# The first stream columns loaded ahead of the last conditioning weights, and the sums of squared keys and queries taken one stream step later

## The chip, the core and the metric

The kernel runs on one core of one Trainium2 chip. The metric is the device time of one execution in microseconds (us). Five engines work side by side, each with a queue of its own: TensorE (PE: matmuls and transposes into PSUM), VectorE (DVE), ScalarE (ACT), GpSimd (POOL) and SyncE (SP, which here issues most of the loads). A semaphore orders two engines where one reads what the other wrote.

## What is computed

One step of a decoder layer for 512 prompt tokens and 8 single tokens of other sequences (520 columns in all), width 1024, in fp32. The part that the change touches:

```
mod  = c @ w_ada + b_ada                       # conditioning: shifts, scales, gates (6 x 1024)
h    = rmsnorm(x, norm1_g) * (1 + sc1) + sh1
proj = h @ w_in                                # q, kv, gates, DeltaNet q/k/v, z, a, b, merge
y    = silu(causal_conv4(DeltaNet q/k/v of proj))
q, k = l2norm(q), l2norm(k)                    # x * rsqrt(sum(x*x) + eps), per head of 128
g    = -exp(a_log) * softplus(a + dt_bias);  beta = sigmoid(b)
o_dn = chunked gated delta rule(q, k, v, g, beta)
o_nsa = native sparse attention (compressed, selected and window branches)
x    = x + gt1 * ((gate_a * o_nsa + gate_b * o_dn) @ w_out)
x    = x + gt2 * (relu(rmsnorm2(x) @ w_up)^2 @ w_down);  then a final rmsnorm
```

## The kernel before, in words

**The stream.** All large products with w_in, w_out, w_up and w_down are cut into units of 128 columns of the weight. A unit is a load of 512 KB (`raw`, `w_load`, L348, issued by SyncE at L351), a rounding on ScalarE (`wh`, L397), a residual on VectorE (`wl`, L401) and two halves of matmuls: the tokens are two halves of 256 and 264 columns, and for each half and each of the eight slices of 128 rows TensorE adds hh·wh, hl·wh and hh·wl (hh and hl are the rounded and the residual part of the normalised input), 24 matmuls into one bank `pg` of PSUM. `load_upto` (L373) issues loads, `split_upto` makes wh and wl, and each call of `step()` first lets every unit in flight go on by one `yield` (`advance()`) and then adds one half to the program. Units in order: two of k_cmp (the first is group 0), the gates, four keys of DeltaNet (k0 to k3), two of v_cmp, keys k4 to k7, eight values, eight queries (q0 to q7), and so on.

**A key or query unit** (`conv`, L556, then `ev_k`, L595, or `ev_q`, L622). Its two halves are copied from PSUM by ScalarE into `pre` (L496); ScalarE multiplies the first tap into `cy` (L565), VectorE adds three taps (L567), ScalarE takes a tanh into `pre` (L569), VectorE makes the silu (L571), and ScalarE squares it into `pre` (L597 for keys, L624 for queries). `norms` (L576) then sums the squares over the 128 rows by four small matmuls (`quarters`; in the profile under L169, `bek<-pre,consts`) into a bank that four heads share; for each fourth head it copies the bank (L587), transposes it, adds EPS on VectorE (L592) and takes the power −1/2 on GpSimd (L593). `pre` and `cy` come from four buffers of one tag (`e2`, L107), with some smaller users.

**Conditioning.** w_ada comes in chunks, two loads of 512 KB a chunk (`ada_load`, L243, issued at L251). The first sixteen are chained: each is issued in SyncE's queue behind the one before (`tc.issue_after(starts[-1].ins)`), and the first stream load behind the sixteenth. `ada` multiplies the conditioning vectors with a chunk (`quarters` again, under L169 as `bek<-wa,consts`), ScalarE copies the result (`ma`, L261), and a second step (`rest`) brings it into `mod` (L267). `modulate` then makes hh and hl of two slices each.

**What sets the order.** A planner lays the queue of each engine: it simulates the program in time and takes what is ready, in the order of the code where several things are, with priorities for some. The place in the code is so a wish and not the order itself.

The loop over the chunks, and what follows it:

```python
    fetch(3)
    for j in range(8):
        ...
        rest.append(ada(i, was[i]))
        fetch(j + 4 if j < 5 else 8)
        ...
    load_upto(0)
    split_upto(0)
```

Of the kernel before, what the change touches and what calls it, by code (L numbers as in the profile page):

```python
# [69 lines left out]
def hybrid_step(ctx: ExitStack, tc: tile.TileContext, A, O, dbg=None):  # L70


    nc = tc.nc
# [19 lines left out]
    def kb4(pool, shape, dt, name, tag, bufs=None):  # L93
        x = pool.tile([128, 2 * SLOT], dt, name=name, tag=tag, **({} if bufs is None else dict(bufs=bufs)))
        n = 1
        for v in shape:
            n *= v
        x = x[:, 0:n]
        return x if len(shape) == 1 else x.rearrange("p (a b) -> p a b", a=shape[0])
# [79 lines left out]
    for hf in range(2):  # L179
        c = slice(hf * 512, hf * 512 + 512)  # L180
        nc.sync.dma_start(crow[hf][0:1], A["c_prompt"][:, c])
        starts = [nc.sync.dma_start(crow[hf][1:9], A["c_sample"][:, c])]
# [62 lines left out]
    def ada_load(j0, hf, pool=None):  # L245
        if pool is None:
            wa = kb4(wp, (4, 256,), F32, "wa", "wraw", bufs=NRAW)
        else:
            wa = kb4(pool, (4, 256,), F32, "wa", "q4")
        with tc.issue_after(starts[-1].ins) if len(starts) < 17 else nullcontext():  # L250
            r = nc.sync.dma_start(wa, w_ada[:, hf * 4:hf * 4 + 4, j0 * 256:j0 * 256 + 256])  # L251
        if len(starts) < 17:
            starts.append(r)
        return wa

    def ada(j0, wa):

        pa = bank("ek")
        quarters(pa[:, 0:256], lambda j, s: cT[:, 18 * j + 9 * s:18 * j + 9 * s + 32], lambda j, s: wa[j // 2][:, j % 2 * 2 + s], True, True, 2)
        ma = e2("ma")[:, 0:256]  # L260
        nc.scalar.copy(out=ma, in_=pa[:, 0:256])  # L261

        def rest():
            pt = bank("ek")
            for hf in range(2):
                mm(pt[:, hf * 16:hf * 16 + 9], ma[:, hf * 128:hf * 128 + 128], sel, start=True, stop=True)
            nc.vector.tensor_tensor(mod[:, 2 * j0:2 * j0 + 2], pt[:, 0:32].rearrange("p (b n) -> p b n", b=2)[:, :, 0:9],  # L267
                                    vec[:, 16 + 2 * j0:18 + 2 * j0, None].to_broadcast([128, 2, 9]), op=ALU.add)
        return rest
# [27 lines left out]
    def norm1(t):  # L297
        n = x_rows(t)[1]
        xt = x_tile(t)
        nc.vector.tensor_scalar(xt[0:n], xt[0:n], ssq[0:n, t:t + 1], None, op0=ALU.mult)  # L300
        for hf in range(2):
            x_transposed(xnT, xt[:, hf * 512:(hf + 1) * 512], t, hf * 4, "sc" if hf else "pt")
# [38 lines left out]
    pos = {"unit": 0, "half": 0, "split": 0, "load": 0}  # L341
# [6 lines left out]
    def w_load(ap):  # L348
        def load():
            raw = kb4(wp, (KT, 128,), F32, "raw", "wraw", bufs=NRAW)  # L350
            nc.sync.dma_start(raw, ap)  # L351
            return raw
        return load

# [18 lines left out]
    def load_upto(g):  # L373
        while pos["load"] <= min(g, len(groups) - 1):
            x = groups[pos["load"]]
            with tc.issue_after(starts[-1].ins) if pos["load"] == 0 else nullcontext():
                x.raw = x.load()
            pos["load"] += 1

    def split_upto(u):  # L380
        while pos["split"] <= u and pos["split"] < len(units):
            un = units[pos["split"]]
            if "ada" in un and pos["split"] > pos["unit"]:
                return
            load_upto(un["g"])
            if un.get("same"):
                un["w"] = un["same"]["w"]
            elif "ada" not in un:
                raw = groups[un["g"]].raw
                if un.get("keep"):  # L390
                    wh, wl = (kb4(wp, (KT, 128,), F32R, "wk", "wkeep", bufs=NKEEP) for _ in range(2))
                else:
                    wh = kb4(wp, (KT, 128,), F32R, "wh", "wh")
                    wl = kb4(wp, (KT, 128,), F32R, "wl", "wl")
                if un["on"] == "scalar":
                    with tc.issue_after(slot["mixed"].ins) if un.get("keep") else nullcontext():
                        nc.scalar.copy(out=wh, in_=raw)  # L397
                else:
                    (nc.vector if un["on"] == "vector" else nc.gpsimd).tensor_copy(wh, raw)
                kp = KT - WLP  # L400
                nc.vector.tensor_tensor(wl[:, 0:kp], raw[:, 0:kp], f32(wh[:, 0:kp]), op=ALU.subtract)  # L401
                if WLP:
                    nc.gpsimd.tensor_tensor(wl[:, kp:], raw[:, kp:], f32(wh[:, kp:]), op=ALU.subtract)
                un["w"] = wh, wl
                load_upto(un["g"] + 2)
            pos["split"] += 1
# [152 lines left out]
    def conv(ct, P, out=None):  # L559

        pre, y = e2("pre"), e2("cy")[:, 0:S]
        nc.vector.memset(pre[:, 0:3], 0.0)
        yield from copies(pre[:, 3:523], P)
        nc.vector.tensor_copy(tail[:, ct], pre[:, 512:523])
        nc.scalar.activation(y, pre[:, 0:S], AF.Copy, scale=cw[:, 0, ct:ct + 1])  # L565
        for j in range(1, 4):
            nc.vector.scalar_tensor_tensor(y, pre[:, j:j + S], cw[:, j, ct:ct + 1], y, op0=ALU.mult, op1=ALU.add)  # L567
        e = pre[:, 0:S]
        nc.scalar.activation(e, y, AF.Tanh)  # L569
        out = y if out is None else out  # L570
        nc.vector.scalar_tensor_tensor(out, e, 1.0, y, op0=ALU.add, op1=ALU.mult)  # L571
        return out, e
# [4 lines left out]
    def norms(i, out, sq):  # L577

        h = i % 4
        if h == 0:  # L580
            norm_bank[0] = bank("ek")
        p = norm_bank[0]
        quarters(p[:, 0:128], lambda j, s: one_of[:, 31 - h:63 - h], lambda j, s: sq[:, j * 128:j * 128 + 128], h == 0, h == 3)
        if h < 3:
            return
        e = e2("nrm")[:, 0:128]
        nc.scalar.copy(out=e, in_=p[:, 0:128])  # L587
        yield
        p = bank("ek")
        tr(p[:, 0:128], e, ident)  # L590
        t = wk.tile([128, 4, 4], F32, name="nsq", tag="nsq", bufs=2)
        nc.vector.tensor_scalar(t, p[:, 0:128].rearrange("p (c h) -> p h c", c=4)[:, 0:4], EPS, None, op0=ALU.add)  # L592
        nc.gpsimd.tensor_tensor(out, t, mhalf.rearrange("p (h c) -> p h c", h=4), op=ALU.pow)  # L593

    def ev_k(i, P):  # L595
        y, e = yield from conv(8 + i, P, slot["kT"][:, i])
        nc.scalar.activation(e, slot["kT"][:, i], AF.Square)  # L597
        yield
        yield
        hs = slice(i - 3, i + 1)  # L600
        r = lns[:, :, hs].rearrange("p c h -> p h c")
        yield from norms(i, r, e)
        if i % 4 == 3:
            nc.vector.tensor_tensor(brk[:, hs], r, slot["beta"][:, :, hs].rearrange("p c h -> p h c"), op=ALU.mult)
            nc.vector.tensor_tensor(brk2[:, :, hs].rearrange("p c h -> p h c"), r, brk[:, hs], op=ALU.mult)
# [16 lines left out]
    def ev_q(i, P):  # L622
        y, e = yield from conv(i, P, slot["qT"][:, i])
        nc.scalar.activation(e, y, AF.Square)  # L624
        yield
        yield
        hs = slice(i - 3, i + 1)
        r = rq2[:, hs]
        yield from norms(i, r, e)
        if i % 4 == 3:  # L630
            nc.vector.tensor_scalar(rq[:, hs], r, float(128 ** -0.5), None, op0=ALU.mult)
            nc.vector.tensor_tensor(r, rq[:, hs], rq[:, hs], op=ALU.mult)
# [95 lines left out]
    g_in("dnk0", C_DN + 1024, 512, ev_k)  # L728
    g_in("v_cmp", C_KV + 256, 256, kv_cmp(2), when("X2"))
    g_in("dnk1", C_DN + 1536, 512, lambda i, P: ev_k(4 + i, P))  # L730
    g_in("dnv", C_DN + 2048, 1024, ev_v, when("bv"))
    g_in("dnq", C_DN, 1024, ev_q, when("bv"))
# [27 lines left out]
    def fetch(n):  # L760

        for j in range(len(was), n):
            i = j // 2 + 4 * (j % 2)
            was[i] = [ada_load(i, 0, q4), ada_load(i, 1, None if j % 4 == 3 else q4)]
# [4 lines left out]
    for j in range(8):  # L769
        if j < 5:  # L770
            norm1(j)
        i = j // 2 + 4 * (j % 2)
        rest.append(ada(i, was[i]))
        fetch(j + 4 if j < 5 else 8)
        if j % 2:
            for r in rest:
                r()
            rest = []
            if j < 4:
                continue  # L780
            for i in range(j // 2 if j > 5 else 0, j // 2 + 1):
                modulate(xnT, 0, 0, 8, hh, hl, 2 * i, 2 * i + 2)
            if j == 5:
                slot["early"] = slot["rest"]
# [1215 lines left out]
```

## Time and profile before

| | us |
|---|---|
| median of three runs | 1309.7 (1305.91 to 1313.38) |
| the profiled execution | 1307.84 |
| its span in the profile | 1306.1 |
| TensorE busy | 1216.6 (93%) |
| VectorE busy | 843.8 (65%) |
| ScalarE busy | 647.2 (50%) |
| GpSimd busy | 230.1 (18%) |

The profile is that of one execution. A row of a view "in order of time" gives the start (us from the beginning of the span), the duration, the engine, the line, the operation, what it writes and reads, and, in brackets, how long the engine sat idle ahead of it and whose end ended that. `bpg` are the banks of the stream, `bek` banks for conditioning, norms and transposes. In a list of stretches PEclk is the clock granted to TensorE as a share of 2.4 GHz: 0.5 is 1.2 GHz.

### The profile page before, as it was taken

How to read it: one execution, taken by the hardware profiler on the slowest of the kernel's cores; microseconds unless marked ns; L12 is line 12 of the kernel's file. 1: busy time of each engine (PE TensorE's matmuls, PEld its weight loads, DVE VectorE, ACT ScalarE, POOL GpSimd, SP SyncE). 2: the span in 40 equal slices, each digit the busy share in tenths (PEclk: the TensorE clock that was granted, in tenths of full speed). 3: DMA queues.
4: the chain of work that ended last, by engine and by line, in shares of the span. 5: the costliest groups of instructions: out<-in, count | busy, mean ns of one | idle time of the engine just before them, and what ended most of it. 6: DMA issues, size and time to landing. Idle time of an engine off the chain costs nothing. (4 is left out here: it accounts for less than half of the span.)

```text
span 1306.1 us, 26716 instructions
## 1 busy us (share of the span) xinstructions
PE 1216.6 (93%) x10356; PEld 1150.1 (88%) x10356; DVE 843.8 (65%) x2291; ACT 647.2 (50%) x1561; POOL 230.1 (18%) x323
## 2 busy tenths in 40 slices
PE   4899899999888999799998899999999999999997
PEld 3788889989788999678887798989999999999996
DVE  4576958795357788787777787896834334334355
ACT  4565857654243336656646677574643132232244
POOL 2112100112111111312221323230431021020000
PEclk9899989999699999899999899999999999999999
DMA  8852412425613345346344222371732332332533
GB/s 273 216 156 74 126 32 51 119 78 151 182 47 108 103 130 146 98 116 197 99 116 136 74 72 85 94 196 33 210 95 69 98 95 83 97 97 83 161 90 105
DMA packets 234834, 149.82 MB, mean 115 GB/s; under 512 B 9290, under 2 KB 230018, under 8 KB 234444
## 3 DMA queue, kind: packets, MB, share of 16 engines
q1 hardware_dynamic: 224804, 134.77, 36.4%
q0 software_dynamic: 2240, 6.38, 1.8%
q10 hardware_dynamic: 7664, 6.97, 1.8%
q8 instruction: 81, 1.33, 0.4%
q14 instruction: 45, 0.37, 0.1%
HBM read 136.87 MB, written 15.60 MB: 117 GB/s over the span
## 5 line engine op out<-in xcount | busy, mean ns | idle before, releaser
L153 PE MATMUL bpg<-hh,wh 128*128 128x256 f32 (+1 forms) x1168 | 342.2, 293 | 1.2 <-ACT hh L1521 0.7
L153 PE MATMUL bpg<-hh,wl 128*128 128x256 f32 (+1 forms) x1168 | 337.5, 289 | 2.0 <-DVE wl L401 2.0
L153 PE MATMUL bpg<-hl,wh 128*128 128x256 f32 (+1 forms) x1168 | 337.7, 289 | 0.0
L153 PEld LDWEIGHTS bpg<-hh,wh 128*128 128x128 f32 x1168 | 225.2, 193 | 5.2 <-issue 2.0
L153 PEld LDWEIGHTS bpg<-hh,wl 128*128 128x128 f32 x1168 | 224.5, 192 | 4.0 <-DVE wl L401 2.5
L153 PEld LDWEIGHTS bpg<-hl,wh 128*128 128x128 f32 x1168 | 225.5, 193 | 1.5 <-issue 0.8
L401 DVE TENSOR_TENSOR wl<-raw,wh 128x1024 fp32r<-128x1024 f32 x149 | 183.0, 1229 | 65.7 <-ACT wh L397 60.3
L397 ACT CAST wh<-raw 128x1024 fp32r<-128x1024 f32 x117 | 121.6, 1048 | 181.9 <-PE bpg L153 174.5
L153 PE MATMUL bpg<-act,wh 128*128 128x264 f32 (+1 forms) x1024 | 186.5, 284 | 0.0
L153 PEld LDWEIGHTS bpg<-act,wh 128*128 128x128 f32 x1024 | 157.7, 188 | 0.1
L153 PE MATMUL bpg<-act,wl 128*128 128x264 f32 (+1 forms) x512 | 145.0, 284 | 0.2 <-DVE wl L401 0.2
L153 PE MATMUL bpg<-h2h,wh 128*128 128x256 f32 (+1 forms) x448 | 126.7, 283 | 0.0
L153 PE MATMUL bpg<-h2h,wl 128*128 128x256 f32 (+1 forms) x448 | 126.6, 282 | 0.0
L153 PE MATMUL bpg<-h2l,wh 128*128 128x256 f32 (+1 forms) x448 | 126.3, 282 | 0.0
L1848 POOL TENSOR_TENSOR r<-r 128x520 f32<-128x520 f32 (+2 forms) x40 | 54.1, 1354 | 291.2 <-ACT r L1847 291.2
L1811 DVE SCALAR_TENSOR_TENSOR o_dn<-bpg,consts,o_dn 128x256 f32<-128x256 f32 x80 | 38.3, 484 | 100.3 <-PE bpg L153 100.3
L153 PEld LDWEIGHTS bpg<-act,wl 128*128 128x128 f32 x512 | 96.5, 189 | 0.5 <-DVE wl L401 0.4
L153 PEld LDWEIGHTS bpg<-h2h,wl 128*128 128x128 f32 x448 | 84.4, 188 | 0.3 <-DVE wl L401 0.2
L153 PEld LDWEIGHTS bpg<-h2l,wh 128*128 128x128 f32 x448 | 84.4, 188 | 0.0
L153 PEld LDWEIGHTS bpg<-h2h,wh 128*128 128x128 f32 x448 | 84.3, 188 | 0.0
L153 PE MATMUL bsp<-K,qst 128*128 128x288 f32 (+6 forms) x288 | 68.9, 317 | 5.5 <-DVE consts L267 2.3
L1851 DVE TENSOR_TENSOR act<-r,act 128x520 fp32r<-128x520 f32 (+2 forms) x40 | 23.6, 590 | 73.4 <-ACT act L1850 73.3
(634 smaller groups left out, 2453.3 us busy)
## 6 DMA issues: line engine op xcount, KB each, us to landing
raw<-in_w_in SPq DMA_DIRECT2D x68, 512.0 KB
wa<-in_w_ada SPq DMA_DIRECT2D x48, 512.0 KB
raw<-in_w_down SPq DMA_DIRECT2D x40, 512.0 KB
raw<-in_w_up SPq DMA_DIRECT2D x36, 512.0 KB
raw<-in_w_out SPq DMA_DIRECT2D x12, 512.0 KB
Sx<-in_state_dn SPq DMA_DIRECT2D x16, 256.0 KB
out_s_dn<-Sx SPq DMA_DIRECT2D x16, 256.0 KB
pg<-in_cache_k_slc SPq DMA_DIRECT2D x16, 128.0 KB
```

Of the source, the lines that this page charges most:

```text
L153: nc.tensor.matmul(out, lhs, rhs, start=start, stop=stop)
L397: nc.scalar.copy(out=wh, in_=raw)
L401: nc.vector.tensor_tensor(wl[:, 0:kp], raw[:, 0:kp], f32(wh[:, 0:kp]), op=ALU.subtract)
L1811: nc.vector.scalar_tensor_tensor(xi[:, q], p[:, 0:n], mod[:, m + i, 0:1], xi[:, q], op0=ALU.mult, op1=ALU.add)
L1848: nc.gpsimd.tensor_tensor(r, r, r, op=ALU.mult)
L1851: nc.vector.tensor_tensor(b_, r, f32(a), op=ALU.subtract)
```

## The change

Two edits. The first moves the load of group 0 in SyncE's queue: it is issued within the loop over the chunks, after `fetch(7)` at j = 3, and takes a place of its own in the chain of the w_ada loads, so that the last two of the sixteen (the halves of the eighth chunk to be fetched) are issued behind it. The split of that unit stays where it was. The second puts one more `yield` ahead of `norms` in `ev_k` and `ev_q`, so that what `norms` issues stands one call of `step()` (half a unit of the stream) later in the program; the squares themselves stay.

```diff
     def w_load(ap):
         def load():
             raw = kb4(wp, (KT, 128,), F32, "raw", "wraw", bufs=NRAW)
-            nc.sync.dma_start(raw, ap)
+            with tc.issue_after(starts[-1].ins) if pos["load"] == 0 else nullcontext():
+                r = nc.sync.dma_start(raw, ap)
+            if pos["load"] == 0:
+                starts[-1] = r
             return raw
         return load
...
             x = groups[pos["load"]]
-            with tc.issue_after(starts[-1].ins) if pos["load"] == 0 else nullcontext():
-                x.raw = x.load()
+            x.raw = x.load()
             pos["load"] += 1
...
         nc.scalar.activation(e, slot["kT"][:, i], AF.Square)
         yield
         yield
+        yield
         hs = slice(i - 3, i + 1)
...
         nc.scalar.activation(e, y, AF.Square)
+        yield
         yield
         yield
...
         fetch(j + 4 if j < 5 else 8)
+        if j == 3:
+            load_upto(0)
         if j % 2:
```

## Rows read from the trace of the kernel before

**Rows 1.** The page's head and its part on engines: busy us, share, instructions.
```profile
span 1306.1 us, 26716 instructions
...
PE 1216.6 (93%) x10356; PEld 1150.1 (88%) x10356; DVE 843.8 (65%) x2291; ACT 647.2 (50%) x1561; POOL 230.1 (18%) x323
```

**Rows 2.** Waits of TensorE, 0 to 75 us: total us, times, longest.
```profile
PE bek L169 <- DMA wa<-in_w_ada: 8.0, 5, 2.9
```

**Rows 3.** Waits of TensorE, 75 to 360 us.
```profile
PE bek L169 <- ACT pre L597: 5.4, 3, 2.5
...
PE bek L169 <- ACT pre L624: 2.2, 1, 2.2
...
PE bsp L160 <- PE bek L169: 0.7, 1, 0.7
```

**Rows 4.** Stretches: us, busy by engine (x count), PEclk, DMA share, GB/s.
```profile
37.00:48.00 11.00, 8.18 (x44) 6.87 (x45) 6.56 (x17) 5.10 (x10) 0.00 (x0) 0.53 1.05 249
48.00:60.00 12.00, 12.00 (x103) 12.00 (x102) 5.97 (x17) 7.92 (x17) 3.01 (x3) 1.00 0.48 130
85.00:89.00 4.00, 4.00 (x23) 3.97 (x21) 4.00 (x11) 2.40 (x4) 1.05 (x1) 0.57 0.32 83
...
140.00:160.00 20.00, 16.13 (x126) 15.02 (x124) 19.46 (x46) 17.42 (x40) 1.83 (x2) 0.91 0.37 105
```

**Rows 5.** SyncE, 27 to 46 us in order of time: start, us, what.
```profile
27.40 5.50 SPq L251 DMA_DIRECT2D wa<-in_w_ada  x6
32.95 4.01 SPq L351 DMA_DIRECT2D raw<-in_w_in  x2
```

**Rows 6.** TensorE, 24 to 49 us in order of time, idle time before in brackets.
```profile
32.58 1.07 PE L169 MATMUL bek<-wa,consts 128*32 128x256 f32 x16 [1.17 <-DMA wa<-in_w_ada]
...
35.85 1.07 PE L169 MATMUL bek<-wa,consts 128*32 128x256 f32 x16 [1.10 <-DMA wa<-in_w_ada]
39.82 1.94 PE L169 MATMUL bek<-wa,consts 128*32 128x256 f32 x16 [2.90 <-DMA wa<-in_w_ada]
...
43.41 0.56 PE L153 MATMUL bpg<-hh,wh 128*128 128x256 f32 x1
```

**Rows 7.** ScalarE and VectorE, 35 to 50 us in order of time.
```profile
42.10 1.05 ACT L397 CAST wh<-raw 128x1024 fp32r<-128x1024 f32 x1
...
43.18 1.22 DVE L401 TENSOR_TENSOR wl<-raw,wh 128x1024 fp32r<-128x1024 f32 x1 [0.26 <-ACT wh L397]
```

**Rows 8.** Norms on TensorE, from its order of time around each.
```profile
102.33 0.42 PE L169 MATMUL bek<-pre,consts 128*32 128x128 f32 x8 [1.37 <-ACT pre L597]
...
263.02 0.42 PE L169 MATMUL bek<-pre,consts 128*32 128x128 f32 x8
...
291.41 0.42 PE L169 MATMUL bek<-pre,consts 128*32 128x128 f32 x8 [2.21 <-ACT pre L624]
```

**Rows 9.** TensorE, 74 to 85 us in order of time.
```profile
75.80 0.28 PE L153 MATMUL bpg<-hh,wh 128*128 128x256 f32 x1
...
84.20 0.43 PE L169 MATMUL bek<-pre,consts 128*32 128x128 f32 x8 [2.50 <-ACT pre L597]
```

**Rows 10.** TensorE's groups by shape, 63.9 to 84 and 269 to 291.7 us.
```profile
L153 PE MATMUL bpg<-hh,wh 128*128 128x256 f32 x24 | 6.8, 282 | 0.0
...
L153 PE MATMUL bpg<-hh,wh 128*128 128x256 f32 x24 | 7.0, 294 | 0.0
```

**Rows 11.** ScalarE, 66 to 90 us in order of time.
```profile
77.66 0.36 ACT L496 COPY pre<-bpg 128x256 f32<-128x256 f32 x1
...
83.52 0.63 ACT L597 ACTIVATE pre<-kT 128x512 f32<-128x512 f32 x1
```

**Rows 12.** VectorE and ScalarE, 259 to 276 us in order of time.
```profile
260.24 0.06 DVE L562 MEMSET pre<- 128x3 f32 x1
...
264.76 0.72 ACT L565 ACTIVATE cy<-pre,consts 128x512 f32<-128x512 f32 x1
```

**Rows 13.** Waits of TensorE, 360 us to the end.
```profile
PE bek L153 <- ACT pth L1495: 5.6, 6, 1.9
```

## The prediction

> **What bounds the kernel now.** I read the shares of the engines first. TensorE is busy 93% of a span of 1306.1 us [rows 1], so only what shortens its idle time, or its time at a low clock, can shorten the whole. The profiled execution took 1307.84 us, 1.7 us more than its span; the median of the three runs, 1309.7, lies 1.9 us above it. The sums below are made against 1307.84.
>
> Next I read the waits of TensorE in the stretches that the change touches. Up to 75 us its wait for w_ada chunks is 8.0 us in five pieces, the longest 2.9 [rows 2]. From 75 to 360 us it waits for the Squares of keys 5.4 us in three pieces and for the Square of a query 2.2 us in one; behind one of them stand 0.7 us more, in which the transposes of xr waited for the norm's matmuls [rows 3]. Of 16 norms (eight keys, eight queries) only these four wait. Part two of the change aims at these 7.6 us (8.3 with the 0.7), part one at the last 2.9 us of conditioning. Together that is 11.2 us, 0.9% of the span.
>
> The clock comes last. From 37 to 48 us the granted clock was 0.53, the level of 1.2 GHz for nearly all of it, and afterwards 1.00; from 85 to 89 us, behind the 2.50 us wait at 84.20, it was 0.57 [rows 4], again mostly 1.2 GHz. That second dip cost (1 − 0.57) × 4 = 1.7 us on top of its wait.
>
> **Part one, the first stream columns ahead of the last w_ada pair.** Nothing is added or removed: the same 512 KB load goes to SyncE's queue two places earlier, and the last two w_ada loads are chained behind it. SyncE issued the last six w_ada loads from 27.40 and the first stream loads from 32.95 [rows 5], so no issue is late: SyncE ran ahead of the data. The order of landing is what changes. The conditioning matmuls, each released by a pair of loads, started at 32.58, 35.85 and 39.82 [rows 6], so a pair takes 3.3 to 4.0 us and one load 1.6 to 2.0. With the stream load ahead, I estimate from these rows that it lands at 37.8 to 38.2 and the last pair at 41.4 to 41.8.
>
> What could TensorE do with it? The cast of the first columns took 1.05 us on ScalarE and the residual 1.22 us on VectorE [rows 7], so wh exists from about 39.1 at best and wl from about 40.4. Of the first unit four matmuls need no wl (two banks, hh and hl against wh). In the kernel before, TensorE is without any gap from 39.82 on: conditioning, then the stream from 43.41 [rows 6]; of 37 to 48 us it is busy 8.18 of 11, which is that one hole and nothing else [rows 4]. In the changed kernel it would start stream matmuls some 0.7 us earlier, run out of them for part of the time until wl is there, and do the late conditioning from 41.6 instead of 39.82. The order of the same work is exchanged; what is won in the 2.9 us hole is bounded by 0.7, and a hole of 0.3 or so may open before wl. The last two of the eight normalised slices come up to 2 us later from the conditioning, but VectorE made wl ahead of them in the kernel before (43.18 [rows 7]) and would have done so already, so most of that is given back. Bounds: −2.9 us (the whole hole filled) and +2.0 us (the whole delay of a load shows); the nearest row is the gapless stretch from 39.82, and I take −0.3.
>
> The clock could move with it. The row shows 0.53 over the 11 us behind the 2.9 us hole. The Trainium skill, "TensorE: Matmul & The Clock Gate", in "What's actually happening" of Part 1, says that the throttled state is the default and that activity releases it. By that rule matmuls in the hole could bring the full clock sooner; the trace agrees as far as it goes, since both dips [rows 4] stand behind an idle stretch, but no run here shows a shorter hole. If it comes sooner by as much as the dip at 85 us cost, it is −1.7 us; if the late pair keeps it low as much longer, +1.7. I take 0.
>
> **Part two, the sums of squares one step later.** An extra yield stands ahead of norms() in ev_k and ev_q, 16 times. No instruction is added. What moves is the place in the code of four matmul calls a head (0.42 us together [rows 8]), and for each fourth head the copy, the transpose, the EPS addition on VectorE and the power on GpSimd. The Squares stay where they were. A step is half a unit, 24 matmuls, 2.95 us: from 75.80 to 81.70 (84.20 less its 2.50 of idle time) two halves ran [rows 9].
>
> By the code of before, the norm of unit n stands ahead of the first half of unit n + 2; now it stands ahead of the second half. But engine queues are laid by the planner, and TensorE's queue shows the result. From 63.9 us, where the first key unit starts, to its norm at 84.20 each kind of 256-column matmul ran 24 times [rows 10], eight a unit: three whole units. So the norm already stands behind BOTH halves of unit n + 2, later than its old place in the code and later than its new one. The same holds for the query norm at 291.41 [rows 8]: 24 from 269 us on. What holds it back is that its Square is ready only then (83.52 [rows 11]), not its place. A planner that puts the norm in when its operand is ready, ahead of the next half whose place in the code is later still (n + 3), does the same with the new code. So I expect these queues to stay as they are: the four waits stay, 7.6 us, and the dip at 85 us with them. Bounds: −10.0 (all of 7.6 + 0.7 + 1.7 won) and the price of the third rival below; I take 0, since the row of the queue is the nearest thing.
>
> The one norm with little delay is that at 102.33 [rows 8]. If it alone goes behind the next half, 1.37 + 0.7 = 2.1 us are to be won at most.
>
> **Sum:** 1307.84 − 0.3 − 0 = 1307.5 for an execution like the profiled one. Half of the distance to the median of the runs (1.9) added, 1308.5 is forecast.
>
> **The rivals.**
> First, the norms do go one half later, as the diff says. Then at 84.20 the next half fills the wait, and it has a bank for that, since there are more than two (the half at 75.80 starts although the first half of the unit before is only copied at 77.66 [rows 9, 11]). −7.6 − 0.7 − 1.7 = −10.0, 1297.8. Of this the wait before 161 us (5.4 − 2.5 − 1.37 = 1.5) is probably not won, as VectorE was busy 19.46 of 20 us there [rows 4]; so −8.5, 1299.3. For it: it is what the code says, and the waits are real. Against it: the queue as it stands [rows 8 to 10].
>
> Second, the hole before 39.82 is filled and the full clock comes sooner: −0.7 − 1.7 = −2.4, 1305.4. For it: both dips follow an idle stretch. Against it: the late pair makes a hole of its own kind behind it.
>
> Third, slower: the `pre` buffer. pre and cy of a unit come from four buffers of one tag, and pre is held until the norm has read it. The norm of query 0 ends at 263.02 + 0.42 = 263.44 [rows 8]; the tap product that fills cy of query 2 starts at 264.76 and pre of that unit was set at 260.24 [rows 12]. A norm one half later ends at 266.39, and the product starts 1.6 us late, and with it that unit's tanh, Square and norm. It hands that on to unit n + 2: three links in the queries (0 to 2, 4, 6), one in each four of keys, five in all, 8.0 us, 1315.8, if the waits stay because the Squares are late too. It decides from the point where the norm comes more than 264.76 − 263.44 = 1.3 us later than now. Against it: it needs the norms to move, which I hold unlikely, and moving them fills waits as well.
>
> Fourth, the planner lays other queues elsewhere since operands come at other times, with no cause in the two edits. The largest group of such waits behind 360 us is 5.6 us in six pieces [rows 13]; taking it as the size gives ±5.6, 1302 to 1314, mostly within what can't be told from no change.
>
> **How the numbers follow.** About 0.5% is what a measurement of this kernel can tell from no change: 6.5 us, so 1303.2 to 1316.2 by the median. Forecast (order unchanged, load exchanged) 0.50; norms later 0.16; clock sooner 0.09; buffers 0.10; other queues 0.15, of which 0.06 fall out on the fast side and 0.05 on the slow side (two such groups, or one on top of another case). Faster: 0.16 + 0.06 = 0.22. Slower: 0.10 + 0.05 and 0.02 for the upper bound of part one on top = 0.17. Same: 0.61. The range goes from 1298.5, which takes in most of the first rival, to 1317, past the third and the bound of +2.0; some 0.15 are left out. The likeliest case alone gives 1305 to 1312.
>
> **What would show it.** In the profile after: the wait at about 84 us and that at 291 us still there, released by the Square, and 48 matmuls of three units ahead of the first norm: the step on the queue is right. If those waits are gone and a half stands there, the first rival. If the last conditioning pair starts at about 41.6 behind stream matmuls and TensorE has no new gap, part one is right; if the granted clock is back before 48 us, the second. If tap products (L565) stand idle behind norms, the third. What would make the prediction wrong most easily is the planner: its order depends on times that no trace shows.

## The result: 17 us slower, and the profile after

The changed kernel took 1329.1 us in the median (1326.07 to 1330.52, four runs), the kernel before 1311.54 (1305.91 to 1315.82) beside it. The recorded ratio is 1.0118, 95% interval 1.0088 to 1.0148, that is 11.5 to 19.4 us; it is not the quotient of the two medians, which would be 1.0134. The forecast was 1308.5, its range ended at 1317. The profiled execution has a span of 1323.6 us, 17.5 more than that of [rows 1]. Four executions of the later sets took 1702 to 2635 us against 1303 to 1332 for all others; they are left out of the ratios and of the clock losses below, and the medians of time move by less than 0.2 us without them.

The page's head and its part on engines, changed kernel:

```profile
span 1323.6 us, 26746 instructions
PE 1228.1 (93%) x10356; PEld 1159.5 (88%) x10356; DVE 842.5 (64%) x2291; ACT 648.0 (49%) x1561; POOL 241.0 (18%) x323
```

The same 10356 matmuls keep TensorE busy 11.5 us longer, and only 6.0 us are more idle time (95.5 against 89.5 by the page). The granted clock accounts for nearly all of the longer busy time. Each run comes with its span and its mean granted clock, and span × (1 − clock) is an estimate of what the lower level cost (it counts idle time at that level too): (1 − 0.961) × 1323.6 = 51.6 us in the profiled execution after, (1 − 0.969) × 1306.1 = 40.5 before, 11.1 us more. The rest of a span is work and idle time:

| | runs | clock loss, median (us) | rest, median (us) |
|---|---|---|---|
| before, beside the first set of experiments | 20 | 45.2 | 1263.8 |
| changed kernel | 4 | 54.4 | 1272.2 |

So about half of the loss is clock: 9.2 us, and 8.4 are waits and work that no longer overlap. (In three later sets the kernel before lost 46.5 to 47.2 us in the median, which would make it 7 to 8.) The prediction had taken the clock at 0, with bounds of 1.7 us.

The places on which the prediction rested come next. Waits of TensorE, changed kernel, 0 to 75 us (total us, times, longest):

```profile
PE bek L169 <- DMA wa<-in_w_ada: 3.3, 2, 2.2
PE bpg L153 <- ACT wh L399: 2.0, 1, 2.0
```

The same view from 75 to 360 us:

```profile
PE bek L169 <- ACT pre L599: 4.4, 3, 2.1
PE bsp L160 <- DVE X L906: 3.7, 2, 2.4
...
PE bek L160 <- DVE cy L573: 1.6, 1, 1.6
```

Against [rows 2, 3]: w_ada waits fell from 8.0 to 3.3 us, and one of 2.0 us for wh came. Three waits for keys' Squares are there again (5.4 became 4.4), but not the same three: 2.13 us at 86.39, 0.23 at 152.38 and 2.01 at 161.19, while that at 102.33 [rows 8] is gone. The one for a query's Square is gone too, and others stand in their place.

TensorE of the changed kernel, 30 to 50 us in order of time:

```profile
37.34 1.94 PE L169 MATMUL bek<-wa,consts 128*32 128x256 f32 x16
41.23 0.58 PE L153 MATMUL bpg<-hh,wh 128*128 128x256 f32 x1 [1.95 <-ACT wh L399]
...
42.39 1.94 PE L169 MATMUL bek<-wa,consts 128*32 128x256 f32 x16
```

ScalarE of the changed kernel in the same stretch:

```profile
39.34 0.37 ACT L261 COPY ma<-bek 128x256 f32<-128x256 f32 x1 [3.30 <-PE bek L169]
39.61 0.62 ACT L327 CAST hh<-xnT 128x512 fp32r<-128x512 f32 x1
40.13 1.05 ACT L399 CAST wh<-raw 128x1024 fp32r<-128x1024 f32 x1
```

Here [rows 6, 7] answer. The last pair of w_ada loads feeds TensorE at 42.39 instead of 39.82. Four stream matmuls, as many as can do without wl, are pushed ahead of it, and they had to wait 1.95 us for wh. Its cast stands on ScalarE behind a cast of hh and behind the copy of a conditioning result, for which ScalarE itself sat idle 3.30 us. When the early load landed no row shows; it was no later than 40.13. The hole of 2.9 us did not fill; it became a hole of 1.95 us with four matmuls and a late pair behind it.

A stretch of the changed kernel (us, busy by engine, PEclk, DMA share, GB/s):

```profile
33.00:50.00 17.00, 14.39 (x87) 10.25 (x88) 7.78 (x22) 5.27 (x11) 0.00 (x0) 0.51 1.11 289
```

The first key norm on TensorE:

```profile
86.39 0.42 PE L169 MATMUL bek<-pre,consts 128*32 128x128 f32 x8 [2.13 <-ACT pre L599]
```

The group of stream matmuls from 66 us to it (busy, mean ns of one, idle time before them):

```profile
L153 PE MATMUL bpg<-hh,wh 128*128 128x256 f32 x24 | 6.8, 282 | 0.0
```

The clock is at 1.2 GHz for 17 us there instead of some 10 [rows 4]; the section on the hardware says why that alone proves little. The norm stands behind 24 matmuls of each kind, three whole units, as in [rows 10], and still waits for its Square (2.13 us, [rows 9]).

**Where the time went.** The n-th stream matmul (the n-th of TensorE's `bpg` rows in order of time) is the same amount of work done in every kernel, so the time between two of them can be compared. The count starts at 0. Lengths in us; "order of before" are executions whose queues in that stretch are those of before (from the kernels below), and "changed" is the changed kernel and after_gp20 (described below), which has its TensorE queue. Each length is from one execution:

| stream matmuls | order of before | changed | difference of the means |
|---|---|---|---|
| start to 288 | 84.3 to 86.8, mean 85.3 (8 executions) | 86.7, 88.0 (mean of 7 with part one: 86.9) | +1.6 |
| 288 to 1152 | 177.4 to 180.9, mean 179.3 (8) | 180.2, 179.9 (mean of 7: 179.4) | +0.1 |
| 1152 to 1536 | 54.4, 54.4, 55.8, 55.9 | 53.1, 53.0 | −2.1 |
| 1536 to 1728 | 102.1, 105.5, 101.2, 103.7 | 101.8, 107.1 | +1.3 |
| 1728 to 2304 | 137.1, 138.3, 138.6, 136.8 | 141.2, 141.2 | +3.5 |
| 2304 to 2688 | 115.8, 116.2, 117.3, 115.8 | 119.4, 119.9 | +3.4 |
| 2688 to 2976 | 98.0, 97.0, 98.0, 97.3 | 97.5, 97.4 | −0.1 |
| 2976 to 3264 | 74.7, 75.0, 77.3, 74.9 | 78.8, 78.9 | +3.4 |
| 3264 to 3648 | 66.6, 66.4, 66.3, 66.4 | 70.1, 69.9 | +3.6 |
| 3648 to the last | 383.8, 383.6, 383.7, 383.4 | 384.4, 384.8 | +1.0 |

The "7 with part one" leave out a_j2, whose load stands elsewhere. The sum is +15.7, near the 17.6 of the medians. Of it 1.6 us lie at the start, where part one works; 14.8 us lie from matmul 1728 on, that is behind 420 us, 100 us later than the last norm that the change touches.

One stretch is shorter: matmuls 1152 to 1536 took 53.0 to 53.1 us in all four executions with the whole change and 54.3 to 56.8 in the twelve others. The norm that waited 2.21 us at 291.41 [rows 8] waits for nothing there:

```profile
292.28 0.43 PE L169 MATMUL bek<-pre,consts 128*32 128x128 f32 x8
```

So part two, on top of part one, did win the query's wait that it aimed at; it was outweighed behind.

### The profile page after: what moved, and what is told of

Its sections match the earlier page's. It is cut to its first block, busy times and chain, and to the rows that moved or that the text cites. A ratio compares the mean times of both kernels' runs of the same rounds, so it can differ in the third digit from the quotient of the medians.

```text
span 1323.6 us, 26746 instructions
## 1 busy us (share of the span) xinstructions
PE 1228.1 (93%) x10356; PEld 1159.5 (88%) x10356; DVE 842.5 (64%) x2291; ACT 648.0 (49%) x1561; POOL 241.0 (18%) x323
## 4 chain that ended last, share of the span: by engine, by line
PE 78%; DVE 8%; DMA 6%; ACT 4%; issue 2%; POOL 1%; SPq 0%; ACTq 0%; POOLq 0%; DVEq 0%
PE bpg L153 54%; PE bsp L153 11%; PE bsp L160 5%; PE bek L153 4%; PE bek L169 3%; DMA wa<-in_w_ada 2%; DVE wl L403 1%; DMA raw<-in_w_up 1%; PE bek L160 1%; DMA Sx<-in_state_dn 1%; DVE X L906 1%; DMA iv<-sc 0%; ACT ps L1470 0%; ACT wh L399 0%; DMA w1r<-in_cmp_w_k 0%
## 5 line engine op out<-in xcount | busy, mean ns | idle before, releaser
L1854 POOL TENSOR_TENSOR r<-r 128x520 f32<-128x520 f32 (+2 forms) x40 | 60.0, 1502 | 287.3 <-ACT r L1853 287.3
L1853 ACT ACTIVATE r<-bpg 128x256 f32<-128x256 f32 (+1 forms) x64 | 24.7, 387 | 137.2 <-PE bpg L153 137.2
L153 PEld LDWEIGHTS bpg<-h2h,wl 128*128 128x128 f32 x448 | 84.3, 188 | 0.0
L153 PEld LDWEIGHTS bpg<-h2h,wh 128*128 128x128 f32 x448 | 84.3, 188 | 0.0
L153 PE MATMUL bsp<-K,qst 128*128 128x256 f32 (+6 forms) x288 | 69.4, 318 | 5.9 <-DVE rounded L1493 1.9
```

What stands on the lines that cost most here:

```text
L153: nc.tensor.matmul(out, lhs, rhs, start=start, stop=stop)
L1853: yield from halves(P, lambda c, p: nc.scalar.activation(r_[:, c], p, AF.Relu), hv)
L1854: nc.gpsimd.tensor_tensor(r, r, r, op=ALU.mult)
```

## The experiments

The ratios are the recorded ones to the kernel before, run beside them on the same chip, with the 95% interval; they differ a little from the quotients of the medians. What is said of the order of queues is read from the built programs and, where a count or a time stands with it, from the traces.

### Part one alone, the last query alone, the keys alone

a_only is the changed kernel without the two yields. The others are the kernel before with one line changed:

```diff
 # q7_only, in ev_q
-        yield
+        yield from ((0, 0) if i == 7 else (0,))
 # keys_only, in ev_k
-        yield
+        yield; yield
```

> Part one alone: the load of group 0 ahead of the last two conditioning loads, norms as before. In the changed kernel the stream is 2 to 3 us late from 60 us to 420 us, and 10 us more are lost behind 440 us. Theory 'start' (the early lateness is that of the last pair and of a longer stretch at half clock, the late loss is that of the query norms): +2 to +3 us on the median, the early lateness there, nothing lost behind 440 us. Theory 'queues of part one' (the other order at the start lets the planner lay all later queues otherwise, and that costs): +10 to +18 us, with waits behind 440 us as in the changed kernel.

> The extra yield for the last query alone (i == 7), nothing else. Theory 'queries' (the norm of the last query, whose place in TensorE's queue does move, sets off the late loss): +8 to +15 us, all of it behind 300 us. Theories 'start' with no part of the queries, and 'queues of part one': within 2 us of before, since nothing ahead of 300 us changes and one norm of 0.42 us moves.

> The extra yield in ev_k alone, for all eight keys. The queues of all five engines come out in the same order as before, so every theory expects 0; what differs from a ratio of 1 is what repeated measurement of one program gives, expected within 0.3%.

| kernel | median, us | ratio | clock loss, median |
|---|---|---|---|
| a_only | 1321.73 | 1.0084 (1.0057 to 1.0110) | 52.1 |
| q7_only | 1321.79 | 1.0082 (1.0048 to 1.0116) | 54.1 |
| keys_only | 1311.81 | 1.0011 (0.9989 to 1.0032) | 45.2 |

For the keys the prediction's step holds to the last instruction: no engine's queue changes. Part one alone and one single yield lose 10 us each, so "start" with 2 to 3 us falls as the whole of it, and "queries" seems to hold for the last query. But look at what moved. TensorE around the last query's norm in the kernel before, in order of time:

```profile
309.45 0.43 PE L169 MATMUL bek<-pre,consts 128*32 128x128 f32 x8
...
310.88 0.60 PE L160 MATMUL bek<-consts,kvt 128*128 128x128 f32 x4
```

And in q7_only:

```profile
309.62 0.60 PE L160 MATMUL bek<-consts,kvt 128*128 128x128 f32 x4
...
311.72 0.43 PE L169 MATMUL bek<-pre,consts 128*32 128x128 f32 x8
```

The norm and four transposes of v_slc, which use banks of the same tag (`bek`), changed places: 0.43 against 0.60 us, with no wait at either. In the traces TensorE's rows differ around 310 to 330 us through this exchange, and then hardly at all up to 548 us; from there to 890 us q7_only's queues are in another order, and the time is lost there: 122.9 us from matmul 2304 to 2688 (115.8 to 117.3 with the order of before) and 79.5 from 2976 to 3264 (74.7 to 77.3). And a_only, whose edit has nothing in common with this one, loses in the same two stretches (120.0 and 78.6) at the same two waits. TensorE, rows with idle time near 664 and 835 us, of q7_only:

```profile
664.11 0.51 PE L153 MATMUL bsp<-K,qst 128*128 128x288 f32 x2 [2.34 <-DVE rounded L1487]
835.71 0.50 PE L153 MATMUL bpg<-hh,wl 128*128 128x256 f32 x1 [1.95 <-DVE wl L401]
```

In the kernel before these two waits are 0.8 and 1.0 us. The same rows of a_only:

```profile
663.97 0.51 PE L153 MATMUL bsp<-K,qst 128*128 128x288 f32 x2 [2.35 <-DVE rounded L1491]
834.14 0.39 PE L153 MATMUL bpg<-hh,wl 128*128 128x256 f32 x1 [2.11 <-DVE wl L403]
```

Two different edits, nearly the same later order of the queues (from 380 to 890 us their TensorE rows differ only near 600 and from 761 to 796 us), and nearly the same loss. That made the order itself the suspect, and the moved instructions only what set it off.

### The load two more places ahead

```diff
-        if j == 3:
+        if j == 2:
             load_upto(0)
```

> Part one with the load of group 0 issued one chunk earlier still (after j = 2), so that four conditioning loads instead of two stand behind it. Theory 'start': TensorE can do no more with the early columns, and two pairs come one load (1.6 to 2.0 us) later; +2 to +5 us, all ahead of 60 us. Theory 'queues of part one': the loss behind 440 us changes at random with another order at the start, anywhere from -6 to +18 us, and does not follow the number of loads passed.

1318.98 us, 1.0062 (1.0040 to 1.0084). With four loads passed instead of two the start took 85.9 us to matmul 288, inside the spread of the order of before. It is one execution, with a granted clock of 0.76 from 30 to 52 us against 0.61 to 0.69 in the others with part one; it shows no loss at the start that grows with the loads passed, and can't exclude one. The clock loss was 46.7 us, hardly more than before; the excess is waits (6.4 us of the 7.4). Another place, another order, another loss: "queues of part one".

### Three more yields, later queues unchanged; and two orders without any edit of loads or norms

```diff
 # q4to6_only, in ev_q; a_q4to6 is a_only with the same line
-        yield
+        yield from ((0, 0) if 4 <= i < 7 else (0,))
 # ya09
-YA = 1.0
+YA = 0.9
 # yn11
-YN = 1.0
+YN = 1.1
```

YA and YN pace the prompt's and the decode attention against the stream. No instruction is added or removed by them.

> The extra yield for three queries of the second four (i = 4, 5, 6), not for the last. Three norms move in TensorE's queue by some matmuls of the same stretch (290 to 310 us) and all queues behind are in the order of before. Theory 'late queues' (what costs is the order that the planner lays behind 480 us, not the moved norms): within 3 us of before, 1308 to 1314, and clock loss as before (about 45 us). Theory 'queries' (a norm that comes later costs by itself): about three times what one moved norm costs in the run for the last query, +10 us or more.

> The kernel before with one constant of the attention stage's pacing at 0.9 instead of 1.0: no load, no norm, no instruction is changed or moved ahead of 480 us; behind it the queues come out in another order. Theory 'late queues, and those of before are a favourable draw': another order loses as well, +3 to +14 us. Theory that only the two edits' own places cost: within 3 us of before, or a gain as often as a loss.

> The kernel before with one constant of the decode attention's pacing at 1.1 instead of 1.0: queues as before up to 557 us, in another order from there to 890 us. Theory 'favourable draw': +2 to +12 us, with more time at the lower clock than before (45 us of loss). Theory of the edits' own places: within 3 us.

> Part one together with the three yields of queries 4, 5 and 6: queues behind 320 us as with part one alone. Theory 'late queues': as part one alone, +8 to +13 us (ratio 1.006 to 1.010). Theory 'queries': that and ten more. Its start is a further execution of part one's start: theory 'start' expects the first key norm at 86 to 88 us, against 84 to 85 in executions of the start of before.

| kernel | median, us | ratio | clock loss | rest |
|---|---|---|---|---|
| q4to6_only | 1311.72 | 0.9989 (0.9966 to 1.0012) | 44.5 | 1263.8 |
| ya09 | 1312.99 | 1.0012 (0.9987 to 1.0038) | 51.1 | 1258.1 |
| yn11 | 1309.19 | 0.9981 (0.9960 to 1.0003) | 50.3 | 1256.4 |
| a_q4to6 | 1320.21 | 1.0067 (1.0045 to 1.0089) | 50.1 | 1265.9 |

The three yields cost nothing, alone or on top of part one. But they test less than was expected of them: in the traces of q4to6_only and a_q4to6 the norms of queries 4 and 5 stand where they stood, and that of query 6 moves by a single stream matmul. These runs say that a yield without another later order is free; what a norm costs that really moves, the kernel q7_ya09 below has to say. The sign expected at the start does not separate either: the first key norm stands at 86.0 us in a_q4to6, and at 84.0 to 86.5 in the eight executions with the start of before.

My next theory fell as well: that the order of before is a favourable draw and any other loses. The two paced kernels have other orders over some 300 us and are the same or 2 us faster. Against the kernel before beside them (46.5 us of clock loss, 1263.6 of rest) yn11 and ya09 lose 3.8 and 4.6 us more to the clock and win 7.2 and 5.5 in the rest.

### The loads that stand ahead in SyncE's queue

In the changed kernel four w_ada loads hold SyncE's queue from 779 to 818 us while stream loads stand behind, and in a_only the wait of 834 us is for a wl. (In the changed kernel itself TensorE has no wait for a wl about 830 us, contrary to the expectation below.) So the last eight w_ada loads were given to GpSimd, in three kernels; TensorE's, VectorE's and ScalarE's queues stay in order.

```diff
-            r = nc.sync.dma_start(wa, ...)
+            r = (nc.gpsimd if 20 <= j0 < 24 else nc.sync).dma_start(wa, ...)
```

> The changed kernel, with the last eight w_ada loads issued by GpSimd instead of SyncE; the queues of TensorE, VectorE and ScalarE keep their order. In the changed kernel four w_ada loads stand in SyncE's queue from 779 to 818 us, waiting for buffers, and stream loads that TensorE needs soon stand behind them; about 830 us TensorE waits for a late wl and then has a stretch at half clock. Theory 'queue head' (these loads hold up the stream): the stretch from 770 to 930 us gets 3 to 7 us shorter, 1322 to 1326 us in all. Theory 'order on the compute engines' (the loss lies in the order of TensorE, VectorE and ScalarE alone): within 2 us of the changed kernel, 1327 to 1331. If GpSimd's own waits for buffers hold up its softmax work instead, slower than the changed kernel.

> Part one alone with the same eight loads on GpSimd. Theory 'queue head': the wait of 2.1 us for wl at 834 us and the half clock behind it (1.7 us) go, 1317 to 1319 us against 1321.7 for part one alone. Theory 'order on the compute engines': 1320 to 1323.

> The kernel before with the same eight loads on GpSimd, the control. There the loads behind were issued at 811 us and no wait for wl follows; theory 'queue head' expects no gain, 1309 to 1313, theory 'order on the compute engines' the same. A gain or a loss here is what the other queue is worth by itself and has to be taken off the two others.

after_gp20 took 1331.79 us (1.0150, 1.0123 to 1.0177), a_gp20 1324.84 (1.0099, 1.0074 to 1.0124), before_gp20 1311.86 (1.0000, 0.9981 to 1.0018). Nothing came back; the first two are even 2.7 and 3.1 us above the kernels without the move, 1 to 2 us above what either theory gave. TensorE near 664 and 834 us in a_gp20:

```profile
661.44 0.56 PE L153 MATMUL bsp<-K,qst 128*128 128x288 f32 x2 [2.35 <-DVE rounded L1491]
...
831.69 0.39 PE L153 MATMUL bpg<-hh,wl 128*128 128x256 f32 x1 [2.10 <-DVE wl L403]
```

The same two waits, 2.35 and 2.10 us, without the loads in front. "Queue head" falls; the loss goes with the order of the compute engines' queues, and it repeats to a tenth of a microsecond where that order repeats (78.8 and 78.9 us from matmul 2976 to 3264 in the table above).

### The same edits under other orders

> The extra yield for the last query, on the kernel whose attention pacing is 0.9. The norm moves by the same rows of TensorE's queue as in the run for the last query alone, but here all five queues behind 320 us come out in the order of that pacing without the yield. Theory 'this order': the yield costs nothing, 1310 to 1316 us as pacing 0.9 alone (1313.0). Theory 'queries' (the later norm costs by itself): 10 us more, 1320 to 1326.

> The changed kernel with the attention pacing 0.9: the same start, the same moved norms, other queues behind 485 us. Theory 'this order' (of the 17 us only the start and the order up to 485 us belong to the change in any case, some 4 to 6 us; the rest is that of one order behind it): the distance to pacing 0.9 alone (1313.0) comes out anywhere from 2 to 20 us and not at 17. Theory 'the two edits cost 17 us wherever they stand': 1328 to 1332.

> The changed kernel with the decode pacing 1.1 (1309.2 us without the change): other queues behind 557 us. Theory 'this order': distance to 1309.2 anywhere from 4 to 20 us, not the same as the 17 of the change and that of pacing 0.9. Theory 'the two edits cost 17 us wherever they stand': 1325 to 1328.

The first is the yield for the last query on ya09. In the traces TensorE's rows differ from those of ya09 only from 308 to 332 us, where norm and transposes change places, and in two rows at 364 us.

| kernel | with the edit | without it | difference |
|---|---|---|---|
| last query's yield, pacing of before | 1321.8 | 1311.6 | +10.2 |
| last query's yield, pacing ya09 | 1312.7 | 1313.0 | −0.3 |
| whole change, pacing of before | 1329.1 | 1311.5 | +17.6 |
| whole change, pacing ya09 | 1322.0 | 1313.0 | +9.0 |
| whole change, pacing yn11 | 1316.6 | 1309.2 | +7.4 |

(The kernel before stood at 1311.5 to 1312.9 beside all of them. Ratios to it: q7_ya09 0.9988, 0.9963 to 1.0013; after_ya09 1.0068, 1.0047 to 1.0088; after_yn11 1.0030, 1.0009 to 1.0052. ya09 and yn11 were measured in an earlier set; with each kernel taken against the kernel before beside it, the three differences under other paces are −1.5, +7.7 and +6.2.)

This settles the norm: the same exchange of norm and transposes costs 10 us where the planner lays the later queues anew, and nothing that can be told from noise where it does not. And it shows that the 17.6 us are not a price of the two edits: under two other paces the whole change costs 6 to 9 us.

What stays in all three is the start (86.7, 86.4 and 86.5 us to matmul 288) and one stretch from 1728 to 2304: 141.2, 140.5 and 141.0 us against 135.0 to 138.6 in the executions without part one. It has one long wait, for a state of the decode path. The waiting matmul on TensorE in the changed kernel:

```profile
459.67 0.43 PE L169 MATMUL bsp<-Sx,dsc 128*32 128x128 f32 x8 [4.26 <-DMA Sx<-in_state_dn]
```

SyncE's queue of the changed kernel ahead of it:

```profile
444.37 8.05 SPq L352 DMA_DIRECT2D raw<-in_w_in  x2
453.08 1.42 SPq L1407 DMA_DIRECT2D out_s_dn<-Sx  x2
454.59 1.84 SPq L1349 DMA_DIRECT2D Sx<-in_state_dn  x2
```

The matmul in the kernel before:

```profile
454.17 0.43 PE L169 MATMUL bsp<-Sx,dsc 128*32 128x128 f32 x8 [0.65 <-DMA Sx<-in_state_dn]
```

SyncE's queue of the kernel before:

```profile
445.60 0.37 SPq L351 DMA_DIRECT2D raw<-in_w_in  x1
447.32 1.42 SPq L1401 DMA_DIRECT2D out_s_dn<-Sx  x2
448.83 1.46 SPq L1343 DMA_DIRECT2D Sx<-in_state_dn  x2
```

After the change SyncE has two stream loads ahead of the state's store and load instead of one, and the second waits until 452 us. TensorE's matmul starts 5.5 us later, 2.0 of which it was late already at matmul 1728, and it waits 4.26 us instead of 0.65.

The kernel with the load two places ahead, which has none of the extra yields, shows the same wait:

```profile
460.74 0.42 PE L169 MATMUL bsp<-Sx,dsc 128*32 128x128 f32 x8 [4.20 <-DMA Sx<-in_state_dn]
```

All sixteen traces divide in this way. In five (the four with the whole change, and a_j2) two stream loads stand ahead of the state, the wait is 4.00 to 4.45 us and the stretch takes 140.5 to 141.2. In the eleven others, a_only among them, one load stands there, the wait is 0.41 to 1.26 us and the stretch takes 135.0 to 138.6. So the 3.5 us of this stretch go with SyncE's order there and are no fixed price of either edit. That the second load is the cause is read from the rows; no kernel changes it alone. The yields for all queries without part one were not tried either.

## Why the prediction was wrong, point by point

**The keys' norms stay where they are: right.** The yields in ev_k alone change no queue, and in the changed kernel each of the eight norms has as many stream matmuls ahead of it as before, the first one those of three whole units (144; the "48 matmuls of three units" of the last paragraph is a slip, 48 is one unit). The waits at 86.39 and 161.19 us are there. That at 102.33 is gone in a_only as well, so by part one and not by the yields: transposes of xr now stand ahead of the norm.

**The queries' norms stay: right for the first four, wrong for the second four.** "So I expect these queues to stay as they are" was concluded from one key and one query norm [rows 10]. Behind both halves of unit n + 2 the last four norms would have 1344, 1392, 1440 and 1488 stream matmuls ahead. In the kernel before they had 1344, 1378, 1415 and 1481: only the one that was read stood where the prediction had them all, and the others stood earlier. In the changed kernel they have 1340, 1380, 1432 and 1488. The last query's norm, whose banks are shared with the transposes of the next units, changes places with four of them even when its yield is the only edit. By itself that cost nothing (−0.3 us on ya09).

**Part one, −0.3 us:** measured +1.6 at the start (means of 7 and 8 executions, whose ranges overlap by 0.5 us), within the bounds but near the upper one. The four matmuls ahead of the late pair came as described; the sum went wrong in the cast, put at 39.1 "at best" and found to end near 41.2, since ScalarE's queue has it behind the conditioning's copy and a cast of hh. TensorE waited for it 1.95 us with the late pair behind.

**The step that failed: "these queues stay as they are", and with it the fourth rival's size.** The forecast rested on later queues that stay in order; they did not, behind part one and behind the last query's norm alike. The fourth rival named the mechanism, "the planner lays other queues elsewhere", but priced it at 5.6 us, one group of waits, with 0.15 of chance and only a third of that on the slow side. What it measured: −2.4 and +1.4 us for two orders laid by another pace; +7.4 (a_j2), +10.1 (a_only), +10.2 (q7_only) and +17.6 us (the change) under the pace of before; +9.0 and +7.4 under the two other paces. In those with part one some 1.6 us are the start. Two things were left out of the term. A new order moves waits over the whole attention stage, not in one group: four stretches between 420 and 929 us lost 3.4 to 3.6 us each. And clock loss comes with it: 9.2 of the 17.6 us.

**The other rivals.** The third (buffers of `pre`) shows no sign: in the changed kernel no tap product of the second four queries stands idle behind a norm. The first came true in a small part: the wait at 291 us is gone in the changed kernel, though its norm has four stream matmuls fewer ahead and not a half more; its Square starts 3.4 us behind the norm of query 3 instead of 8.8. The 2.2 us are less than what was lost elsewhere. The second is turned round: the clock came back later (50 us, not 48). That need not be the change, as the section on the hardware shows.

**What stays open:** why orders behind the change lose and the two paced ones do not. Six of six losing is less than it sounds, since a_only and q7_only share most of the order in which they lose. A common start is not the reason, as q7_only has that of before. No run here separates a common cause from chance.

## What to carry to other kernels

Where a planner lays the queues, a change has two prices: its own, and that of the order that it sets off, which can be many times as large and lie hundreds of microseconds behind; compare the built queues before reasoning about the first. Count the place of every instance that an edit touches, not of one: here one norm of the last four stood where the rule drawn from it had all. An edit that leaves every queue in order cost nothing here (keys_only, q4to6_only), and one that changes the order of a late stage has to be judged under two or three paces before it is called good or bad in itself. Compare stages by equal work done, and split each run into clock loss and rest: in the two paced kernels they moved against each other.

## What the runs showed of the hardware

One program does not get the same clock every time. The start up to 300 us has the same queues in before, keys_only, q4to6_only and q7_only; the stretch from 30 to 52 us stands below for before (us, busy by engine, PEclk, DMA share, GB/s); the granted clock there is 0.69 in keys_only and in q4to6_only:

```profile
30.00:52.00 22.00, 16.83 (x138) 13.56 (x138) 12.44 (x40) 7.72 (x18) 0.00 (x0) 0.77 0.93 255
```

For q7_only:

```profile
30.00:52.00 22.00, 18.74 (x132) 14.09 (x132) 13.35 (x45) 8.20 (x21) 0.00 (x0) 0.61 0.97 273
```

The mean granted clock went from 0.77 to 0.61 with no difference in what TensorE was given, an estimated 3.5 us of TensorE time ((0.77 − 0.61) × 22). The changed kernel's 0.61 in the same stretch need be no effect of the change, then. Over a whole execution of the kernel before the clock loss ran from 37.8 to 49.9 us in 20 runs, while the rest stayed between 1259.7 and 1268.1; in 28 runs on another chip it went up to 59.2. The profiled execution of before, at 0.969, was one of the least throttled, (1 − 0.969) × 1306.1 = 40.5 us, so a single pair of profiles can overstate or understate a change by some 5 us.

TensorE can also be at the lower clock with hardly a wait ahead. In the kernel before, from 331 to 345 us:

```profile
331.00:345.00 14.00, 14.00 (x299) 10.95 (x291) 4.49 (x9) 2.49 (x5) 1.89 (x2) 0.51 0.39 121
```

The granted clock is 0.51, TensorE is busy throughout, and its only wait from 320 us on is one of 0.46 us. What it ran just before, and for part of the stretch, are products of 32x32 and 64x64 blocks (194 of the 32x32 matmuls stand in the stretch).

The Trainium skill, "TensorE: Matmul & The Clock Gate", "What's actually happening" in Part 1, says that activity releases the throttle. The runs agree in that most low stretches stand behind waits, but the same waits did not bring the same stretches each time, and the stretch from 331 us stands behind next to none.
